# Softmax rows scaled by VectorE instead of GpSimd, and two sets of weight low parts moved the other way

## The chip, the core and the metric

The kernel runs on one core of a Trainium2 chip. Times are device microseconds of one execution of the whole program. Five engines work side by side, each through its own list of instructions in order, and wait for each other by semaphores: TensorE (PE; its weight loads are PEld), VectorE (DVE), ScalarE (ACT), GpSimd (POOL) and SyncE (SP), which issues the DMAs.

## The reference

Two decoder layers on a sequence of 512 tokens with 1024 channels, in float32. Each layer normalises x, projects it once, and runs three groups of causal attention on the parts of the projection:

```python
s = einsum(q, k) * ATTN_SCALE            # 4 forgetting heads, 8 sparse heads, 4 dilated heads
p, _ = masked_softmax(s, mask)           # e / sum(e)
o = einsum(p, v)
o = gb[..., 0:1] * o_c + gb[..., 1:2] * o_s + gb[..., 2:3] * o_w     # the sparse heads: gated sum of three branches
```

The sparse heads have a compressed branch (32 windows of keys and values go through a small MLP with the weights `cmp_w1` and `cmp_w2`), a selected branch and a window branch. With 512 tokens every block is selected and the window covers all, so both run over full causal rows. The heads' outputs are concatenated, multiplied by `w_out`, normalised and added to x. Then comes a gated MLP with a causal convolution, normalised and added likewise.

## The kernel before

**Products in parts.** Every float32 operand of TensorE is parted into a high part, rounded to the type that TensorE takes, and a low part, the rest; a product is three matmuls (high by high, high by low, low by high). For weights `part_weights` (L136) does it: ACT writes the high part of a chunk (L145), and a subtraction writes the low part, raw minus high. It runs on POOL (L149) for the chunks named in `ONPOOL` (L30) and on DVE (L153) for the others, `w1` (compression weights, 16 chunks of 128x1024) and `wo` (the first half of the output weights, 8 chunks) among these. Both cut such a chunk into two halves of 128x512. `plan` lists all chunks in the order of use, and `getw` (L201) asks for the load and the parting of a chunk some chunks ahead of its use (one ahead for these, `PRE`).

**The softmax part.** The full rows (4 forgetting heads, 8 sparse heads with two branches each, 4 dilated heads, each in four tiles of 128 queries: 24 x 4 = 96 units per layer) run as a pipeline of stages, one unit to a slot. The unit of tile t has rows of n = 128(t+1) keys. The stages, with the engine that works and the lag in slots behind the scores:

- `st_scores`: TensorE, two or three matmuls into a bank `s` of PSUM (two banks).
- `st_max`, lag 1: DVE adds the mask and takes the row minimum of the negated scores (L1073), into a row `r` in SBUF; this frees the bank.
- `st_exp`, lag 1: ACT takes the exponential of the row and its sum (L1078).
- `st_norm`, lag 2: DVE takes the reciprocal of the sum (L1083), and POOL multiplies the row by it and by the gate (L1085; by 1.0 where a head has no gate).
- `st_turn`, lag 4: TensorE turns the row's blocks over into a bank `pt` (L1096; two banks).
- `st_keep_hi` and `st_keep_lo`, lag 5: ACT writes the high part of the turned weights (L1113), DVE the low part `pl` (L1118); this frees the bank.
- `st_values` and `st_out`, lag 7: TensorE multiplies with the values into a bank `o` (one bank), ACT and DVE evacuate it (L1153, L1154).

Between the slots' stages TensorE runs pieces of the other projections, of the compression MLP and of the first half of the output projection (`main_pieces`, `cmp_pieces`), 1.4 pieces to a slot at first and 0.8 later. TensorE's order is written out by hand; the other engines' order comes from a scheduler that places instructions by its own estimate of when their inputs are there. DVE also adds up the rotary embedding (L446), POOL also writes low parts of the mixed heads (L642).

Before this part stand the first projections, behind it the rest of the output projection, the norms and the MLP.

Of the kernel before, what the change touches and what calls it, by code (L numbers as in the profile page):

```python
# [13 lines left out]
ALU = mybir.AluOpType  # L14
# [14 lines left out]
TAIL = 4  # L29
ONPOOL = ("dv", "dq", "dk", "ks", "nq0", "kw", "kc", "nq1",  # L30
          (0, "fk", 0), (0, "fk", 1), ("up", 0, 1), ("up", 0, 2), ("up", 0, 3), ("up", 1, 0))
# [9 lines left out]
FIRST = 5  # L41
DCUTS = ("w1", "wo")
EV = (1, 3, 1, 1)
# [30 lines left out]
def tile_hybrid_block(  # L74
# [6 lines left out]
    nc = tc.nc  # L81
# [46 lines left out]

# [1 line left out]
    def load(srcs, nk, ncol, tagn=""):  # L130
# [67 lines left out]
    where = {p[0]: i for i, p in enumerate(plan)}  # L198
    done = [0, 0]

    def getw(*key, ahead=AHEAD, pre=None, peek=False):  # L201
        """the parts of a chunk; has those up to `ahead` after it loaded and those up to `pre` after it parted"""
        i = where[key]
        pre = ahead if pre is None else min(pre, ahead)
        tag = lambda k: "_".join(str(z) for z in k)
        for n in range(len(done)):
            upto = i + (ahead, pre)[n]
            while done[n] < len(plan) and done[n] <= upto:
                k, srcs, nk, ncol, spare = plan[done[n]]
                if n == 0:  # L210
                    ready[k] = load(srcs, nk, ncol, tag(k))
                else:
                    ready[k] = part_weights(ready[k], nk, ncol, spare, tag(k), k[1] in ONPOOL or k[1:4] in ONPOOL or k[0:3] in ONPOOL,
                                            k[1] in DCUTS)
                done[n] += 1
        return None if peek else ready.pop(key)

# [1 line left out]
    epsc = const.tile([128, 1], F32, name="epsc")  # L219
# [4 lines left out]
    def table(func, after):  # L224
        """has the function's table loaded once `after` is there"""
        t = st(1, "tb")
        nc.scalar.activation(t, after, func, scale=0.0, bias=onec)
# [17 lines left out]

    # gains of the pre norms, a channel to a partition: they are applied to the turned rows
    pre_g = const.tile([128, 2, DEPTH, KT], F32, name="preg")
# [7 lines left out]
    def turn_pair(half, i, l, tags, tilewise=False):  # L255
        """two token tiles of h, turned over, times the gains, in two parts"""
        gain = pre_g[:, i, l, :]
        pts = [ps(tag) for tag in tags]
        order = [(k, i) for k in range(KT) for i in range(2)]
        for k, i in sorted(order, key=lambda z: z[1]) if tilewise else order:  # L260
            nc.tensor.transpose(pts[k // 2][:, 256 * (k % 2) + 128 * i:256 * (k % 2) + 128 * i + 128],
                                hs[2 * half + i][:, 128 * k:128 * k + 128], ident)
        for k in range(KT):
            src = pts[k // 2][:, 256 * (k % 2):256 * (k % 2) + 256]
            hi, lo = (z[k // 2][:, k % 2, 256 * half:256 * half + 256] for z in hT)
            nc.scalar.activation(hi, src, AF.Copy, scale=gain[:, k:k + 1])  # L266
            nc.vector.scalar_tensor_tensor(lo, src, gain[:, k:k + 1], f(hi), op0=ALU.mult, op1=ALU.subtract)  # L267

    # post norm, residual and pre norm, in stages, two token tiles at a time
    xs, hs, stats = [], [], {}  # L270

    def post_sq(s, halves, gain, engs, then=None):
        """squares of a token tile, and its products with the gains (the last of them after `then`)"""
        if s % 2 == 0:
            stats["p", s // 2], stats["x", s // 2] = st(4, "sq"), st(2, "sx")
        hs.append(bt([128, DM], name="h"))
        scr = rt()
        for u, y in enumerate(halves):
            cs = slice(512 * u, 512 * u + 512)
            c = 2 * u + s % 2  # L280
            nc.scalar.activation(scr, y, AF.Square, accum_out=stats["p", s // 2][:, c:c + 1])  # L281
            if u == 1 and then is not None:
                then()
            (nc.gpsimd if (s, u) in engs else nc.vector).tensor_mul(hs[s][:, cs], y, gain[:, cs])
# [80 lines left out]

# [1 line left out]
    posi = small.tile([128, NST], I32, tag="posi", bufs=1, name="posi")  # L367
# [57 lines left out]
    for l in range(DEPTH):  # L425
        # ================= mixer =================
        table(AF.Exp, hs[3][:, 0:1])
# [55 lines left out]

# [1 line left out]
        bias = small.tile([128, 28], F32, tag="gbias", bufs=1, name=nm("gbias"))  # L485
# [39 lines left out]
        if l == 0:  # L525
# [3 lines left out]
            nc.vector.tensor_scalar(utri, ui, 0.0, None, op0=ALU.is_ge)  # L529
            # selectors of the forget rows: ones on partitions h and 32 + h  # L530
            pcol = small.tile([128, 4], F32, tag="pc", bufs=1, name="pcol")
# [9 lines left out]

        # log sigmoid(z) = min(z, 0) - log(1 + exp(-|z|))
        lz = zz[:, :, 0:4]
# [41 lines left out]
        if l == 0:  # L585
# [1 line left out]
            dint = rt(dt=I32)  # L587
# [18 lines left out]
            for v, lg in ((2.0, -math.log(2.0)), (3.0, -math.log(3.0))):  # L606
                t = rt()
                nc.vector.tensor_scalar(t, cnt, v, lg, op0=ALU.is_equal, op1=ALU.mult)
                nc.vector.tensor_add(dmask, dmask, t)
            # compressed blocks: valid where q - (16 n + 31) >= 0  # L610
            ci = rt((128, NST, 32))
# [5 lines left out]
            nc.vector.tensor_scalar(cinv, ci, 0.0, BIG, op0=ALU.is_lt, op1=ALU.mult)  # L617
            # heads of a pair: ones on the partitions (32 n ..) of even or of odd n
            odd = const.tile([128, 2], F32, name="odd")
# [24 lines left out]
        def o_mms(o, s, ks, w, first, last):  # L644
            """w: for each of ks its two parts, [128, 1, columns]"""
            sl = slice(128 * s, 128 * s + 128)
# [5 lines left out]

# [1 line left out]
        class Pieces:  # L654
            """`main` pieces in their order; a piece may put off work by some pieces (`later`)"""

# [18 lines left out]
        def proj256(name, evac, after):  # L675
            """[s, 256] columns of w_in, two token tiles to a bank; evac(s, psum) then after()"""
            pp = [ps("acc"), ps("acc")]
# [11 lines left out]
        def staged(key, turned, dup, nh, v=None, plain=0):  # L689
            """evac and after of a group: heads side by side (twice when dup), then turned over"""  # L690
            tl = []
# [34 lines left out]
        def main_pieces():  # L726
            # compressed keys and values
            tl = []
# [84 lines left out]

            # output projection, first its part over the full heads
            for k in OFIRST:
# [19 lines left out]
        def merge(a, b):  # L835
            """two pieces of a to one of b"""
            live = True
# [7 lines left out]

        # the other part of the output projection, over the sparse heads
        ch, po = {}, {}
# [45 lines left out]
        def cmp_pieces(xc, w2r):  # L893
            # gelu and second compression product
            t1, t2 = rt((128, 256)), rt((128, 256))
# [60 lines left out]
            yield  # L956
            # compressed attention weights of all sparse heads
            nq = store["nq"]
# [73 lines left out]

# [1 line left out]
        units = []  # L1034
# [46 lines left out]
        def st_norm(u):  # L1081
            n, row, sm_ = u["n"], u["row"], u["sm"]
            nc.vector.reciprocal(sm_[:, 2:3], sm_[:, 1:2])  # L1083
            g_ = 1.0 if u["gate"] is None else gates[:, u["t"], u["gate"]:u["gate"] + 1]
            nc.gpsimd.tensor_scalar(row[:, 0:n], row[:, 0:n], sm_[:, 2:3], g_, op0=ALU.mult, op1=ALU.mult)  # L1085

        def st_turn(u):
            if u["t"] == 0:
                state["r"] = u["row"]
                return  # L1090
            # the first two tiles of rows share a bank
            blocks = [state["r"][:, 0:128]] if u["t"] == 1 else []
# [67 lines left out]
        def cmp_values(k):  # L1160
            """adds the compressed branch to heads 2k, 2k + 1, both at once"""
            p = ps("pt")
# [22 lines left out]
        with tc.manual_schedule(engines={mybir.EngineType.PE}):  # L1185
# [16 lines left out]
            while whole or live[0] or pieces.late:  # L1202
                if whole and store.get("pc"):
                    cmp_values(whole.pop(0)[0])
                elif live[0] or pieces.late:
                    step()
                    chain_step()
# [1 line left out]
            out_mms(2, (7,), True, (0,))  # L1209
# [28 lines left out]

        # ================= MLP =================
        cw = lambda j, c: cpar[:, j // 2, 44 * (j % 2) + c:44 * (j % 2) + c + 1]  # L1240
# [100 lines left out]
```

## Time and profile before

| | |
|---|---|
| Median of 3 runs | 1392.79 us (1392.07 to 1394.44) |
| Profiled execution, from its first to its last instruction (span) | 1390.7 us |
| TensorE busy | 1343.5 us (97%) |
| DVE busy | 873.2 us (63%) |
| ACT busy | 728.1 us (52%) |
| POOL busy | 311.5 us (22%) |
| Granted TensorE clock, mean | 0.997 |

The page gives the profiled execution's own time as its span; the time of a run also holds what lies around the span. The median lies 2.1 us above the span of the profiled execution. Busy time is the time in which at least one instruction of the engine is in work. A wait is written as the engine and line that waited, an arrow, and what released it. The tile names are the program's: `wl_w` is the low part of a chunk of compression weights, `wl_wo` one of output weights, `pl` a low part of turned softmax weights, `r` a softmax row, `sm` its statistics. The softmax part lies at 70 to 312 us in layer 0 and some 684.6 us later in layer 1.

### The profile page before, as it was taken

Reading aid. Unit: us, or ns where it says so; the run is one execution under the profiler, and the core shown is the slowest. Engines: PE = TensorE matmul, PEld = TensorE weight load, DVE = VectorE, ACT = ScalarE, POOL = GpSimd, SP = SyncE. Lnnn points to the kernel's source line nnn. Section 1 sums busy time; section 2 is a strip of 40 time slices with the busy share of each in tenths; the row PEclk is TensorE's granted clock in tenths of the full one; section 3 lists DMA queues with packets and bytes.
Section 4 is the critical chain, followed back from the end, with each engine's and each line's share of the span. In section 5 each row is a group of like instructions: output and inputs, shape, how many; then the busy total and the mean of one; then the engine's idle time right before and its main releaser. Section 6 shows DMA issues by size and latency. Waiting matters only on the chain.

```text
span 1390.7 us, 21646 instructions
## 1 busy us (share of the span) xinstructions
PE 1343.5 (97%) x8019; PEld 1186.6 (85%) x8019; DVE 873.2 (63%) x2022; ACT 728.1 (52%) x1541; POOL 311.5 (22%) x363
## 2 busy tenths in 40 slices
PE   6999999999999999999999999999989999999997
PEld 6899999987888888888899899999878888888886
DVE  6678778678655555433464887876767555554334
ACT  6567767775443333422465677677755333333222
POOL 1363663345000000000004646633430000000000
PEclk9999999999999999999999999999999999999999
DMA  5223311132233333223323142112313333332231
GB/s 178 77 62 110 108 47 41 50 111 74 75 93 93 104 92 102 96 91 121 118 85 107 47 126 88 32 47 62 107 61 101 97 91 106 92 100 97 91 121 61
DMA packets 145521, 123.78 MB, mean 89 GB/s; under 512 B 8264, under 2 KB 135688, under 8 KB 145416
## 3 DMA queue, kind: packets, MB, share of 16 engines
q1 hardware_dynamic: 145416, 122.40, 29.1%
q8 instruction: 63, 1.03, 0.3%
q14 instruction: 42, 0.34, 0.1%
HBM read 118.19 MB, written 4.19 MB: 88 GB/s over the span
## 4 chain that ended last, share of the span: by engine, by line
PE 79%; DVE 11%; ACT 5%; issue 2%; POOL 1%; DMA 1%; SPq 0%; DVEq 0%; ACTq 0%; POOLq 0%
PE acc L114 35%; PE s L114 17%; PE pt L114 13%; PE o L114 10%; PE pt L1096 3%; DVE wt L771 1%; DVE r L1073 1%; DVE hl L267 1%; DVE x L301 1%; DVE r L446 1%; ACT r L1078 1%; ACT r L281 1%; DMA raw_fv<-in_w_in_dram 1%; DVE pl L1118 1%; ACT hh L266 0%
## 5 line engine op out<-in xcount | busy, mean ns | idle before, releaser
L153 DVE TENSOR_TENSOR wl_up<-raw_up,wh_up 128x1024 fp32r<-128x1024 f32 x78 | 95.5, 1225 | 163.2 <-ACT wh_up L145 163.2
L145 ACT ACTIVATE wh_up<-raw_up 128x1024 fp32r<-128x1024 f32 (+1 forms) x90 | 89.6, 1002 | 156.2 <-PE acc L114 68.2
L153 DVE TENSOR_TENSOR wl_wd<-raw_wd,wh_wd 128x1024 fp32r<-128x1024 f32 x42 | 51.5, 1225 | 133.6 <-ACT wh_wd L145 133.6
L1078 ACT ACTIVATE r<-r,sm 128x128 f32<-128x128 f32 x192 | 107.0, 558 | 25.6 <-DVE sm L1073 22.7
L145 ACT ACTIVATE wh_wd<-raw_wd 128x1024 fp32r<-128x1024 f32 x42 | 44.5, 1060 | 144.9 <-PE pt L114 135.6
L1085 POOL TENSOR_SCALAR r<-r,sm,gates 128x128 f32<-128x128 f32 (+3 forms) x128 | 84.1, 662 | 118.6 <-DVE sm L1083 95.9
L149 POOL TENSOR_TENSOR wl_kc<-raw_kc,wh_kc 128x512 fp32r<-128x512 f32 x8 | 11.3, 1426 | 419.7 <-ACT wh_kc L145 419.7
L114 PE MATMUL acc<-hl,wh_up 128*128 128x512 f32 (+1 forms) x272 | 102.6, 377 | 0.0
L114 PE MATMUL acc<-hh,wh_up 128*128 128x512 f32 (+1 forms) x272 | 102.6, 377 | 0.0
L114 PE MATMUL acc<-hh,wl_up 128*128 128x512 f32 (+1 forms) x272 | 102.5, 377 | 0.0
L114 PE MATMUL s<-k,q 128*128 128x512 f32 (+3 forms) x384 | 98.8, 338 | 2.3 <-DVE k L467 1.0
L1118 DVE TENSOR_TENSOR pl<-pt,ph 128x384 fp32r<-128x384 f32 x144 | 85.5, 594 | 10.2 <-ACT ph L1113 9.1
L1073 DVE CUSTOM_DVE_ANT_0 r<-s,cmask 128x128 f32<-128x128 f32 (+3 forms) x160 | 75.5, 482 | 19.3 <-PE s L114 13.8
L1113 ACT ACTIVATE ph<-pt 128x384 fp32r<-128x384 f32 x144 | 75.3, 523 | 21.3 <-PE pt L1096 19.5
L1096 PE MATMUL pt<-ident,r 128*128 128x128 f32 x480 | 77.2, 275 | 6.8 <-DVE pl L1118 3.3
L114 PE MATMUL acc<-wh_wd,gh 128*128 128x512 f32 x252 | 83.8, 389 | 0.0
L114 PE MATMUL s<-hh,wh_up 128*128 128x512 f32 (+1 forms) x224 | 80.7, 360 | 0.4 <-DVE hl L267 0.4
L114 PE MATMUL s<-hl,wh_up 128*128 128x512 f32 (+1 forms) x224 | 80.4, 359 | 0.0
L114 PE MATMUL s<-hh,wl_up 128*128 128x512 f32 (+1 forms) x224 | 80.4, 359 | 0.0
L1265 ACT ACTIVATE r<-r 128x512 f32<-128x512 f32 x44 | 27.8, 632 | 81.3 <-DVE r L1246 81.0
L114 PE MATMUL o<-ph,v 128*128 128x256 f32 (+1 forms) x288 | 69.6, 270 | 0.4 <-DVE mx L1154 0.4
L114 PE MATMUL o<-pl,v 128*128 128x256 f32 (+1 forms) x288 | 67.2, 282 | 1.9 <-DVE pl L1118 1.7
(431 smaller groups left out, 4227.7 us busy)
## 6 DMA issues: line engine op xcount, KB each, us to landing
raw_up<-in_w_up_dram SPq DMA_DIRECT2D x88, 512.0 KB, 3.8
raw_wd<-in_w_down_dram SPq DMA_DIRECT2D x44, 512.0 KB, 3.5
raw_wo<-in_w_out_dram SPq DMA_DIRECT2D x16, 512.0 KB, 3.5
x<-in_x_dram SPq DMA_DIRECT2D x8, 512.0 KB, 6.7
raw_nq<-in_w_in_dram SPq DMA_DIRECT2D x8, 512.0 KB, 3.8
raw_w<-in_cmp_w_k_dram SPq DMA_DIRECT2D x8, 512.0 KB, 3.7
raw_w<-in_cmp_w_v_dram SPq DMA_DIRECT2D x8, 512.0 KB, 3.7
raw_fk<-in_w_in_dram SPq DMA_DIRECT2D x4, 512.0 KB, 7.1
```

What stands on the lines that cost most here:

```text
L114: nc.tensor.matmul(o, lhsT=lhsT, rhs=rhs, start=start, stop=stop, skip_group_check=True)
L145: nc.scalar.activation(hi[:, ks], raw[:, ks], AF.Copy)
L153: nc.vector.tensor_sub(lo[:, ks], raw[:, ks], f(hi)[:, ks])
L267: nc.vector.scalar_tensor_tensor(lo, src, gain[:, k:k + 1], f(hi), op0=ALU.mult, op1=ALU.subtract)
L281: nc.scalar.activation(scr, y, AF.Square, accum_out=stats["p", s // 2][:, c:c + 1])
L1073: nc.vector.tensor_tensor_reduce(row[:, 0:n], u["S"][:, 0:n], u["mask"][:, 512 - n:512], op0=ALU.add, op1=ALU.min, scale=1.0, scalar=3.0e3 ...
L1078: nc.scalar.activation(row[:, 0:n], row[:, 0:n], AF.Exp, scale=-1.0, bias=sm_[:, 0:1], accum_out=sm_[:, 1:2])
L1085: nc.gpsimd.tensor_scalar(row[:, 0:n], row[:, 0:n], sm_[:, 2:3], g_, op0=ALU.mult, op1=ALU.mult)
L1096: nc.tensor.transpose(p[:, 128 * b:128 * b + 128], src, ident)
L1113: nc.scalar.activation(hi, src, AF.Copy)
L1118: nc.vector.tensor_sub(*u["lo"])
L1265: nc.scalar.activation(cd[0], cd[0], AF.Silu)
```

## The change

`st_norm` has DVE multiply the row, directly behind its reciprocal, where POOL did it. `w1` and `wo` are put into `ONPOOL`, so that POOL makes their low parts in two halves, as DVE did before; `DCUTS`, which had DVE cut these two, is emptied. Comments are taken out elsewhere.

```diff
-ONPOOL = ("dv", "dq", "dk", "ks", "nq0", "kw", "kc", "nq1",
+ONPOOL = ("w1", "wo", "dv", "dq", "dk", "ks", "nq0", "kw", "kc", "nq1",
...
-DCUTS = ("w1", "wo")
+DCUTS = ()
...
-            nc.gpsimd.tensor_scalar(row[:, 0:n], row[:, 0:n], sm_[:, 2:3], g_, op0=ALU.mult, op1=ALU.mult)
+            nc.vector.tensor_scalar(row[:, 0:n], row[:, 0:n], sm_[:, 2:3], g_, op0=ALU.mult, op1=ALU.mult)
```

TensorE's instructions keep their order. On DVE, in the last heads of layer 0 (the dilated ones, about 288 to 296 us before; `r` with a number is the row of one unit, `sm` its statistics, `mx` the sum of a pair of heads), the order changes as follows:

```order
 L1083 RECIPROCAL sm_4240<-sm_4240 128x1
-L1083 RECIPROCAL sm_4256<-sm_4256 128x1
 L1073 ISA r_4283,sm_4284<-s_4249,dmask 128x384
 L1073 ISA sm_4284 128x1
+L1085 TENSOR_SCALAR r_4239<-r_4239,sm_4240 128x128
 L1154 TENSOR_TENSOR mx_4089<-o_4148,r_4274 64x512
 L1118 TENSOR_TENSOR pl_4281<-pt_4270,ph_4280 128x3x128
+L1083 RECIPROCAL sm_4256<-sm_4256 128x1
 L1073 ISA r_4307,sm_4308<-s_4277,dmask 128x512
 L1073 ISA sm_4308 128x1
+L1085 TENSOR_SCALAR r_4255<-r_4255,sm_4256 128x256
```

Each row's scaling stands on DVE some instructions behind its reciprocal, and a later reciprocal has moved behind a low part `pl`.

On POOL, in the stretch where the compression hidden layer runs in layer 0 (about 124 to 145 us before; `wl_w_0_0` and the like are low parts of compression weights, `wl_kw` one of a projection):

```order
-L1085 TENSOR_SCALAR r_1411<-r_1411,sm_1412 128x512
-L1085 TENSOR_SCALAR r_1449<-r_1449,sm_1450 128x128
-L1085 TENSOR_SCALAR r_1486<-r_1486,sm_1487 128x256
+L149 TENSOR_TENSOR wl_w_0_0_275_1556<-raw_w_0_0_234_1380,wh_w_0_0_274_1555 128x512
 L642 TENSOR_TENSOR mix_1508<-mx_1318,mix_1508 128x512
-L1085 TENSOR_SCALAR r_1538<-r_1538,sm_1539 128x384
-L1085 TENSOR_SCALAR r_1641<-r_1641,sm_1642 128x512
+L149 TENSOR_TENSOR wl_w_0_1_282_1597<-raw_w_0_1_273_1553,wh_w_0_1_281_1596 128x512 x2
 L149 TENSOR_TENSOR wl_kw_296_1685<-raw_kw_280_1594,wh_kw_295_1684 128x512 x2
```

The scalings have left POOL's queue, and what stands there now are subtractions of weights and of mixed heads alone.

## Rows read from the trace of the kernel before

**Rows 1.** Page: head, and busy time of each engine.

```profile
span 1390.7 us, 21646 instructions
...
PE 1343.5 (97%) x8019; PEld 1186.6 (85%) x8019; DVE 873.2 (63%) x2022; ACT 728.1 (52%) x1541; POOL 311.5 (22%) x363
```

**Rows 2.** Busy time by stretch: length, then each engine; the two softmax parts.

```profile
70.00:312.00 242.00, 233.53 (x1844) 222.56 (x1843) 188.95 (x618) 175.06 (x470) 122.48 (x152) 1.00 0.25 74
755.00:997.00 242.00, 232.06 (x1832) 220.92 (x1831) 189.20 (x608) 173.46 (x464) 122.22 (x152) 1.00 0.25 73
```

**Rows 3.** Waits of TensorE: total us, times, longest.

```profile
PE pt L712 <- DVE pl L1118: 4.7, 4, 2.5
PE pt L1096 <- DVE pl L1118: 3.3, 2, 1.7
PE pt L1096 <- DVE sm L1083: 2.2, 2, 1.2
PE pt L114 <- DVE pl L1118: 2.0, 2, 1.0
```

**Rows 4.** Groups of instructions: busy us, mean ns of one | idle before.

```profile
L153 DVE TENSOR_TENSOR wl_w<-raw_w,wh_w 128x512 fp32r<-128x512 f32 x32 | 23.9, 762 | 0.0
L153 DVE TENSOR_TENSOR wl_wo<-raw_wo,wh_wo 128x512 fp32r<-128x512 f32 x16 | 13.0, 826 | 0.1
...
L149 POOL TENSOR_TENSOR wl_nq<-raw_nq,wh_nq 128x512 fp32r<-128x512 f32 x16 | 20.5, 1291 | 17.9 <-ACT wh_nq L145 17.7
```

**Rows 5.** POOL's scalings (L1085) by stretch, layer 0.

```profile
70.00:312.00 242.00, 60.34 (x96) 1.00 0.25 74
90.00:110.00 20.00, 4.38 (x8) 1.00 0.25 77
150.00:210.00 60.00, 14.64 (x25) 1.00 0.24 70
284.00:306.00 22.00, 9.01 (x16) 1.00 0.16 49
```

**Rows 6.** Groups of instructions, by form: DVE's tensor by scalars within SBUF.

```profile
L605 DVE TENSOR_SCALAR dmask<-r 128x512 f32<-128x512 f32 x1 | 0.4, 415 | 0.0
L615 DVE TENSOR_SCALAR cvalid<-r 128x128 f32<-128x128 f32 x1 | 0.2, 219 | 0.0
```

**Rows 7.** Busy time by stretch: PE, PEld, DVE, ACT, POOL; DVE's fullest stretches.

```profile
90.00:110.00 20.00, 18.69 (x152) 18.02 (x152) 17.49 (x54) 13.11 (x38) 13.16 (x14) 1.00 0.25 77
150.00:210.00 60.00, 58.05 (x480) 56.48 (x479) 47.09 (x172) 42.09 (x118) 40.31 (x54) 1.00 0.24 70
284.00:306.00 22.00, 18.89 (x127) 16.00 (x126) 18.53 (x61) 20.69 (x55) 14.02 (x20) 1.00 0.16 49
```

**Rows 8.** The same stretches, DVE's compression weight lows alone, and their sum.

```profile
90.00:110.00 20.00, 1.60 (x2) 1.00 0.25 77
...
sum 102.00, DVE 1.60; mean DVE 0.53
```

**Rows 9.** Timeline of DVE and POOL, single places: start, us, instruction.

```profile
152.30 0.22 DVE L446 TENSOR_TENSOR r<-rope,rope 128x64 f32<-128x64 f32 x1
...
112.09 1.10 DVE L446 TENSOR_TENSOR r<-rope,rope 128x64 f32<-128x64 f32 x1
...
111.82 1.28 POOL L642 TENSOR_TENSOR mix<-mx,mix 128x512 fp32r<-128x512 f32 x1 [1.80 <-ACT mix L641]
...
329.13 1.42 DVE L319 TENSOR_SCALAR h<-x,sm 128x1024 f32<-128x1024 f32 x2
...
329.98 4.17 POOL L149 TENSOR_TENSOR wl_up<-raw_up,wh_up 128x512 fp32r<-128x512 f32 x3 [2.36 <-ACT wh_up L145]
```

**Rows 10.** Chain of waits, 284 to 312 us: start, us, what.

```profile
287.34 1.15 issue
288.49 1.27 POOL r L1085 x2
...
291.07 0.57 DVE pl L1118
```

## The prediction, made before the changed kernel ran

> **What bounds the kernel now.** I read the head of the page first. The span is 1390.7 us, TensorE is busy for 1343.5 us of it, DVE for 873.2 and GpSimd (POOL) for 311.5 [rows 1]. So little is to be won: nothing in the change touches a matmul, and only the 47 us in which TensorE is idle can shrink. The change works in the softmax part of each layer, so I next asked for busy time in the two stretches that hold it: 242 us per layer, TensorE 233.5 and 232.1 us, DVE 189.0 and 189.2, POOL 122.5 and 122.2 [rows 2]. The layers are copies of each other to a few tenths; I work on layer 0 and double. Then the waits of TensorE: what ends them in this part is almost always DVE, mostly its low parts `pl` (4.7, 3.3 and 2.0 us); only 2.2 us in two waits stand against the reciprocal, that is, against the normalisation behind it [rows 3]. So the normalisation as such is rarely late. What makes TensorE wait is DVE, an in-order engine, being behind with everything.
>
> **The change, part by part.** DVE loses the low parts of 32 chunk halves of the compression weights (23.9 us) and 16 of the output weights (13.0 us): 36.9 us in all, 18.5 per layer. POOL loses 192 scalings and gains these 48 subtractions. It takes 1.29 us for a subtraction of 128x512 (the `wl_nq` row, the same shape) [rows 4], so it gains 62 us; the 96 scalings of layer 0 alone are 60.3 us [rows 5]. DVE gains the 192 scalings. DVE runs the same form, a tensor by scalars within SBUF, once at 128x128 in 0.22 us and at 128x512 in 0.415 [rows 6]. On the line between them 128x256 is 0.284 and 128x384 0.349; the four shapes are equally frequent, so the mean is 0.317 us, 30.4 us per layer. That is 11.9 us more DVE work per layer than is taken off, on 189. Spread evenly this would fit into 242 us. It does not come evenly: the weight lows sit where TensorE works through the compression hidden layer and the output projection, the scalings sit wherever rows run.
>
> So I sum DVE over the stretches where it is fullest [rows 7], with the scalings that begin there [rows 5]:
> - 90 to 110 us: 17.49 busy, less two weight lows (1.60 [rows 8]), plus 8 x 0.317 = 2.5: 18.4 of 20.
> - 150 to 210 us: 47.09 busy, no weight low to lose [rows 8], plus 25 x 0.317 = 7.9: 55.0 of 60.
> - 284 to 306 us, the last heads, where few projection matmuls are left as filling: 18.53 plus 16 x 0.317 = 5.1: 23.6 of 22. Here the work alone is 1.6 us over the stretch. ACT is at 20.69 of 22 there and stays so.
>
> **The shared port** is the unknown cost. In the trace, DVE's rope sum of 128x64 takes 0.22 us at 152.3; at 112.1 it takes 1.10, and it ends with a POOL subtraction that began 0.27 us earlier and lasts 1.28 [rows 9]. So a DVE instruction with two SBUF inputs stands still until POOL's is through. For the form that the change adds no row shows DVE being held; the nearest is the scaling of 128x1024 at 329.1: there three POOL subtractions that start in the middle of it take 4.17 us instead of 3 x 1.29 = 3.87, so one of them was held by it for some 0.3 us [rows 9]. I bound the price: from nothing (DVE's scaling never waits) to a full hold in the order of arrival, that is the share of time in which POOL is busy after the change, times half a subtraction (0.65 us). POOL's remaining work is 13.16 - 4.38 + 2 x 1.29 = 11.4 of 20 us (57%), 25.7 of 60 (43%) and 5.0 of 22 (23%) [rows 5, 7]. That gives 8 x 0.57 x 0.65 = 3.0, 25 x 0.43 x 0.65 = 7.0 and 16 x 0.23 x 0.65 = 2.4 us. Below nothing the bound hardly goes: what POOL's scalings now hold up on DVE is in the busy time of the stretches already, and I leave it there. I take half of the upper end, since one row shows the hold at full length, the other only a third of a microsecond, and that on the other engine.
>
> The Trainium skill speaks against this change. In "SBUF — State Buffer", section "Who interferes with whom", it says that DVE and GpSimd share one pair of SBUF ports as an exclusive lock held for the whole instruction, and that a `tensor_scalar` in a two-port mode takes it as much as an operation with two SBUF inputs does; "VectorE: DVE Perf Modes", section "Mode 2×_2P", puts an fp32 `tensor_scalar` within SBUF into that mode. The rope row agrees for two inputs; that DVE's scaling is held too, no row shows. By this rule the full hold would apply and the time would be that of rival 1 below, 1414.6 us; if the scaling never waits, only the last stretch overflows, by 1.6 us less the 0.8 worked out below, and the time would be 1392.8 + 2 x 0.8 = 1394.4 us.
>
> **What of it reaches TensorE.** With half the hold DVE has 19.9 us to do in 20, 58.5 in 60 and 24.8 in 22. In the first two it fits only if DVE never waits for an input, and now it is idle for 2.5 of 20 and 12.9 of 60. The score, transpose and value banks give TensorE a slot or so of freedom, so I take 0.5 and 1.5 us. In the last stretch the excess is 2.8; on the other side the chain there now goes through two of POOL's scalings for 1.27 us, which stand behind a weight low in POOL's queue (the 1.15 us put down as issue), and then through DVE's row minimum and low part [rows 10]. On DVE two scalings take 0.4 to 0.8 us; I set 0.8 us against the excess: 2.8 - 0.8 = 2.0. Sum 4.0 us per layer, 8.0 in all.
>
> What I cost at nothing: the lows of the compression and output weights on POOL take 2.6 us per chunk instead of 1.5. They are asked for one chunk ahead, and POOL in all does less (122.5 - 60.3 + 24 x 1.29 = 93 of 242 us), and no longer stands in its queue waiting for reciprocals. If that cover fails, TensorE waits for a `wl_w` or `wl_wo`, up to 1.3 us a chunk. The MLP, the first projections and the post norms have no instruction of the change in them.
>
> The sum: 1390.7 + 8.0 = 1398.7 us for the span. The median of the runs, 1392.8, lies 2.1 us above the profiled span; with the same 2.1 the forecast is **1400.8 us**.
>
> **Rivals.**
> 1. *The lock in full.* DVE is 1.4, 2.0 and 4.0 us over in the three stretches, and in the last one the 3.5 us in which it waits for ACT and TensorE do not fill up either: 10.9 per layer, 1392.8 + 21.8 = 1414.6 us. For it: the rope row. Against it: POOL's work thins out to 23% just where DVE is fullest. Chance 0.12. (The rule of "SBUF — State Buffer", section "Who interferes with whom", in the Trainium skill would have it so.)
> 2. *Faster: the queue behind the reciprocal goes.* Place: the end of the softmax part and the transposes that wait for rows. POOL, in order, now holds weight lows and mix lows behind scalings that wait for DVE, and scalings behind weight lows; afterwards each engine only queues its own. Price: at best half of TensorE's waits on `pl` and on the reciprocal, 4.7 + 3.3 + 2.2 + 2.0 = 12.2 us [rows 3], so 1392.8 - 6 = 1386.8 us. It decides if DVE's scalings fit into the 3.5 us that DVE is idle in 284 to 306, that is, if they cost under 0.22 us each. For it: part of DVE's idle time there is the wait for the very chain that gets shorter. Against it: DVE is what TensorE waits for, and it gets more work. Chance 0.18.
> 3. *No change.* The extra DVE work falls into its idle time and the banks' slack, and the shorter chain at the end pays for the excess of 1.6: 1392.8 us. For it: without the lock only the last stretch overflows. Chance 0.13.
>
> **How the numbers follow.** My forecast has 0.57, with 1396 to 1409 as its own range: no hold and 1.6 us per layer at the low end, nearly the full hold at the high end. A measurement of this kernel can tell about 0.2% (2.8 us) from no change. Slower is the forecast and rival 1: 0.69; same is rival 3: 0.13; faster is rival 2: 0.18. The range that should hold 8 in 10 has to reach past no change on one side and to rival 1 on the other: 1388 to 1414 us.
>
> **What would show it.** Right: DVE's busy time in the softmax part rises by 12 to 25 us per layer; some of the new scalings take about 1 us instead of 0.2 to 0.4 and end with a POOL subtraction; TensorE's waits on DVE grow most between 284 and 306 us and their counterpart 684.6 us later. Wrong: scalings that all keep 0.2 to 0.4 us (no hold for this form); a softmax part no longer than 242 us with DVE over 200 us busy in it (slack larger than I think); TensorE waiting for `wl_w` or `wl_wo`; or a difference in the MLP.

## The result, and the profile after

The changed kernel takes 1425.72 us (median of 4 runs, 1423.93 to 1427.69) against 1393.62 us for the kernel before in the same session: a ratio of 1.0226, 95% interval 1.0209 to 1.0243. It is slower, as forecast, but by 32 us where 8 had been forecast, and the time lies outside the range of 1388 to 1414.

The head of the page of the kernel after, to be held against [rows 1]:

```profile
span 1425.9 us, 21291 instructions
...
PE 1356.4 (95%) x8019; PEld 1195.4 (84%) x8019; DVE 942.5 (66%) x2166; ACT 730.5 (51%) x1541; POOL 254.8 (18%) x219
```

TensorE issues the same 8019 matmuls in the same order. DVE's busy time has grown by 69.3 us; the prediction's terms give 36 (scalings 60.8, less lows 36.9, plus half the hold, 12.4). POOL has shrunk by 57. TensorE's own busy time has grown by 12.9.

Since TensorE's order is unchanged, the n-th matmul of one trace is the n-th of the other, and the two softmax parts can be cut at the same instructions. Busy time by stretch (length, PE, PEld, DVE, ACT, POOL, granted clock), those parts of the kernel after, 260.5 and 258.0 us long where [rows 2] has 242 each:

```profile
70.60:331.10 260.50, 240.27 (x1843) 226.75 (x1843) 223.99 (x690) 176.42 (x470) 94.12 (x80) 0.98 0.23 68
774.10:1032.10 258.00, 237.03 (x1831) 224.12 (x1830) 222.97 (x679) 174.33 (x464) 94.27 (x80) 0.99 0.23 68
```

Nearly all of the loss is in these two parts: the delay of the n-th matmul is 0.5 us at the head of the first, 19.1 at its end, 19.0 at the head of the second, 35.0 at its end and 35.2 near the end of the program. (The two profiled executions lie 35.2 us apart, the medians 32.) DVE is busy for 224 and 223 us there, 34 to 35 more than before (12 to 25 were to show the prediction right); POOL for 94 (the prediction has 93). In two of the three stretches the prediction worked with, the delay grows by 5.2 (90 to 110 us of the trace before) and 5.7 us (150 to 210), in the third by 3.6 (284 to 306). The prediction has 0.5, 1.5 and 2.0, and wanted the largest growth in the third.

The scalings on DVE, by form (busy us, mean ns); `gates` among the inputs means two operands of one value per partition, `sm` alone means one:

```profile
L1085 DVE TENSOR_SCALAR r<-r,sm,gates 128x512 f32<-128x512 f32 x32 | 22.8, 714 | 0.8
...
L1085 DVE TENSOR_SCALAR r<-r,sm,gates 128x128 f32<-128x128 f32 x32 | 16.7, 523 | 0.7
...
L1085 DVE TENSOR_SCALAR r<-r,sm 128x384 f32<-128x384 f32 x16 | 11.5, 722 | 0.3
...
L1085 DVE TENSOR_SCALAR r<-r,sm 128x128 f32<-128x128 f32 x16 | 5.6, 348 | 0.4
```

[Rows 6] had promised 415 ns at 512 columns and 219 at 128. Two things lie on top. One is in every scaling: where no POOL instruction is in work beside it, the median at 128, 256, 384 and 512 columns is 285, 352, 420 and 477 ns with one per-partition operand and 345, 412, 480 and 543 with two. Over the 192 that is a mean of 0.425 us. The other is the hold: 44 of the 192 begin while a POOL instruction runs. For a scaling that meets a POOL instruction I call excess what it takes beyond the unheld median of the same form plus 40 ns (a margin for the scatter); the sum is 23.9 us. By the same count the rope sums (L446) rise from 12.7 us of excess to 23.3.

Where it hurts most, at 92 to 102 us, rows from the timeline of the kernel after (start, us, engine, instruction, idle before and what ended it):

```profile
91.96 1.28 POOL L778 TENSOR_TENSOR wth<-wt,wth 128x512 fp32r<-128x512 f32 x1 [2.99 <-ACT wth L777]
...
92.01 1.46 DVE L1085 TENSOR_SCALAR r<-r,sm 128x384 f32<-128x384 f32 x1
...
94.70 3.20 POOL L771 TENSOR_TENSOR wt<-r,posT 64x496 f32<-64x496 f32 x2
...
96.72 1.33 DVE L446 TENSOR_TENSOR r<-rope,rope 128x32 f32<-128x32 f32 x2
...
97.98 1.28 POOL L149 TENSOR_TENSOR wl_kw<-raw_kw,wh_kw 128x512 fp32r<-128x512 f32 x1
...
98.16 1.87 DVE L771 TENSOR_TENSOR wt<-r,posT 64x496 f32<-64x496 f32 x1
...
101.83 1.11 PE L712 MATMUL pt<-ident,r 128*128 128x128 f32 x4 [2.94 <-DVE pl L1118]
```

The same place of the kernel before:

```profile
90.69 1.40 DVE L446 TENSOR_TENSOR r<-rope,rope 128x32 f32<-128x32 f32 x2
...
92.63 1.48 DVE L771 TENSOR_TENSOR wt<-r,posT 64x496 f32<-64x496 f32 x1
```

The scaling of 384 columns starts 0.05 us behind POOL's subtraction and takes 1.46 us instead of 0.42; then a rope sum and a window sum are held too, and with everything behind them late TensorE stands still for 2.94 us. In the kernel before a rope sum and a window sum are held at this place as well, and TensorE stands still for 1.3 us; new here are the scalings. The row `pl` names the last thing it waited for, not the cause.

TensorE's waits in the kernel after (total us, times, longest), against [rows 3]:

```profile
PE pt L712 <- DVE pl L1118: 6.6, 4, 2.9
...
PE pt L1096 <- DVE sm L1083: 5.5, 4, 3.1
PE s L114 <- DVE sm L1073: 5.4, 6, 1.6
PE pt L1096 <- DVE pl L1118: 4.6, 4, 1.3
PE pt L1096 <- DVE r L1085: 3.5, 4, 1.4
PE acc L994 <- DVE r L973: 2.9, 2, 1.5
```

These are DVE's, and all that grew are, but for 0.9 us on POOL's `r` (L988). No wait is for a `wl_w` or `wl_wo`, and only 3.5 us are for the scaling itself.

A part of the loss may be TensorE's clock. The column before the last two of a stretch is the granted clock; the first four rows are of the kernel after, the two behind them of before:

```profile
101.00:107.80 6.80, 5.97 (x25) 5.58 (x26) 5.55 (x17) 5.53 (x13) 1.50 (x2) 0.50 0.20 68
240.90:244.30 3.40, 3.40 (x19) 3.40 (x18) 2.50 (x10) 3.08 (x8) 1.72 (x2) 0.50 0.51 154
...
804.10:807.50 3.40, 3.40 (x17) 3.33 (x16) 3.31 (x9) 3.01 (x8) 0.31 (x1) 0.50 0.00 0
1002.10:1005.50 3.40, 3.40 (x16) 3.40 (x17) 3.36 (x13) 1.96 (x5) 1.28 (x1) 0.50 0.02 6
```

```profile
331.50:334.90 3.40, 3.40 (x19) 3.40 (x18) 3.01 (x8) 3.40 (x11) 3.40 (x4) 0.50 0.18 51
101.00:107.80 6.80, 6.80 (x57) 6.47 (x56) 6.13 (x19) 4.93 (x14) 2.47 (x3) 1.00 0.26 91
```

In or right behind stretches in which TensorE was kept waiting (the first fall lies in the wait of 2.94 us above; the longest stall ahead of each of the six falls is 0.7 to 3.1 us), the chip grants 0.50 (1.2 GHz) instead of 1.00 (2.4 GHz). Leaving out the very end of the program, the kernel before has 3.4 us of this, the kernel after 23.9 us in six places (22.84 us of it TensorE is busy). If the 19.4 us of additional busy time at half clock would have taken half at full clock, this is up to 9.7 us of the 32. Time at half clock does not tell the loss by itself: the runs below with the lows alone and with no scaling have 13.7 and 10.2 us of it, and are 2 and 3 us slower than the kernel before.

### The profile page after: what moved, and what is told of

The parts are those of the page before. It is cut to its first block, busy times and chain, and to the rows that moved or that the text cites. A ratio compares the mean times of both kernels' runs of the same rounds, so it can differ in the third digit from the quotient of the medians.

```text
span 1425.9 us, 21291 instructions
## 1 busy us (share of the span) xinstructions
PE 1356.4 (95%) x8019; PEld 1195.4 (84%) x8019; DVE 942.5 (66%) x2166; ACT 730.5 (51%) x1541; POOL 254.8 (18%) x219
## 4 chain that ended last, share of the span: by engine, by line
PE 72%; DVE 19%; ACT 5%; issue 2%; DMA 1%; SPq 0%; POOL 0%; ACTq 0%; DVEq 0%; POOLq 0%
PE acc L114 32%; PE s L114 16%; PE pt L114 12%; PE o L114 8%; DVE r L1085 3%; PE pt L1096 2%; DVE pl L1118 2%; DVE r L1073 2%; DVE r L446 1%; DVE q L460 1%; DVE hl L267 1%; DVE x L301 1%; DVE wt L771 1%; PE pt L712 1%; ACT r L281 1%
## 5 line engine op out<-in xcount | busy, mean ns | idle before, releaser
L1073 DVE CUSTOM_DVE_ANT_0 r<-s,cmask 128x128 f32<-128x128 f32 (+3 forms) x160 | 75.5, 482 | 10.2 <-PE s L114 9.8
L1096 PEld LDWEIGHTS pt<-ident,r 128*128 128x128 f32 x480 | 56.0, 142 | 26.1 <-DVE pl L1118 8.1
L1085 DVE TENSOR_SCALAR r<-r,sm,gates 128x128 f32<-128x128 f32 (+3 forms) x128 | 71.4, 564 | 3.0
L114 PEld LDWEIGHTS s<-k,q 128*128 128x128 f32 x384 | 60.4, 195 | 12.2 <-DVE sm L1073 6.7
```

The costliest lines, as they stand in the source:

```text
L114: nc.tensor.matmul(o, lhsT=lhsT, rhs=rhs, start=start, stop=stop, skip_group_check=True)
L1073: nc.vector.tensor_tensor_reduce(row[:, 0:n], u["S"][:, 0:n], u["mask"][:, 512 - n:512], op0=ALU.add, op1=ALU.min, scale=1.0, scalar=3.0e3 ...
L1085: nc.vector.tensor_scalar(row[:, 0:n], row[:, 0:n], sm_[:, 2:3], g_, op0=ALU.mult, op1=ALU.mult)
L1096: nc.tensor.transpose(p[:, 128 * b:128 * b + 128], src, ident)
```

## The experiments

Ratios are to the kernel before, run on the same chip, with 95% intervals; a difference between two experiments is taken from their ratios times 1394 us. "Excess" is the sum described above. Two explanations are set against each other: by the load theory VectorE's added busy time makes TensorE late, by the hold theory its single operations that are held behind GpSimd's do.

One thing is not the same in all runs. The scheduler places the other engines' instructions anew for each kernel. With the weight lows and the scalings left out of the count, some 60 of VectorE's 1830 stand in another place in the run without scalings than in the kernel after, and 26 in the run with six reciprocals. No run tells what the new order costs by itself.

**One part of the change at a time.** The scalings alone on VectorE (the weight lows as before), and the weight lows alone on GpSimd (the scalings as before):

```diff
 e1_scale_only: before, with
-            nc.gpsimd.tensor_scalar(row[:, 0:n], row[:, 0:n], sm_[:, 2:3], g_, op0=ALU.mult, op1=ALU.mult)
+            nc.vector.tensor_scalar(row[:, 0:n], row[:, 0:n], sm_[:, 2:3], g_, op0=ALU.mult, op1=ALU.mult)
 e2_lows_only: before, with
-ONPOOL = ("dv", ...
+ONPOOL = ("w1", "wo", "dv", ...
-DCUTS = ("w1", "wo")
+DCUTS = ()
```

> The scalings alone are on VectorE; the low parts of the compression and output weights stay there too, as before. Load theory (VectorE's added busy time makes TensorE late): VectorE carries the scalings' free 82 us (192 at 0.425 us mean, from the run after) and gives none of the 36 us of weight lows back, so this is the slowest of the three, about 1440 us. Hold theory (VectorE's operations are held behind GpSimd's 1.3 us subtractions): 48 subtractions of 1.3 us are gone from GpSimd, the scalings' excess over their free price falls from 24 us to about 12, and the time falls below the run after, to about 1412 us.

> The weight lows alone are on GpSimd; the scalings stay there too. Load theory: VectorE sheds 36 us of the before run's 873 and TensorE is no later, 1385 to 1394 us. Hold theory: 48 more subtractions hold VectorE's other operations (rope sums 12.7 us of excess before, 23 after), about 1398 us. Third: GpSimd's own queue, 312 us busy before and 374 now, makes scalings late, and TensorE waits for them: 1400 us or more, with waits of the transposes L1096 for GpSimd's L1085.

Measured: scalings alone 1421.41 us, 1.0195 [1.0178, 1.0212]; lows alone 1396.18 us, 1.0014 [1.0005, 1.0023]. The loss comes with the scalings; moving the lows alone costs 2 us. That lies nearest to the hold theory's 1398: the rope sums' excess rises from 12.7 to 17.4 us. With the scalings alone the excess is 18.7 us in the scalings (12 was expected) and 9.9 in the rope sums, so the hold theory had the sign right (4 us faster than the run after, with intervals that just touch, though DVE has 36 us more of weight lows) and the size too large. The load theory's 1440 fell. DVE is busy for longer than in the run after, and the time is shorter:

```profile
PE 1356.0 (95%) x8019; PEld 1196.7 (84%) x8019; DVE 951.0 (67%) x2214; ACT 731.1 (51%) x1541; POOL 193.8 (14%) x171
```

**The scaling without its per-partition operands.** The run after with

```diff
-            nc.vector.tensor_scalar(row[:, 0:n], row[:, 0:n], sm_[:, 2:3], g_, op0=ALU.mult, op1=ALU.mult)
+            nc.vector.tensor_scalar(row[:, 0:n], row[:, 0:n], 0.5, 1.0, op0=ALU.mult, op1=ALU.mult)
```

> The run after with the reciprocal and the gate left out of the scaling, which multiplies by two constants in their place, the instruction and its place kept. Price theory (each operand that is read from a partition's scalar costs about 65 ns): the scaling falls to 0.219 us at 128 columns and 0.415 at 512, VectorE loses 320 x 65 ns = 21 us, and the time falls by about half of that, to 1415 us. Hold theory: the excess of the scalings behind GpSimd stays at about 24 us and the time at 1420 us or above.

Measured: 1412.92 us, 1.0143 [1.0128, 1.0158]. The view of the line shows the shortest and median scaling:

```profile
L1085 DVE TENSOR_SCALAR r<-r x192: 197/340/1470, 71.3 to 1011.6; 128x128 f32<-128x128 f32 x48, 128x256 f32<-128x256 f32 x48, 128x384 f32<-128x384 f32 x48, 128x512 f32<-128x512 f32 x48
```

Unheld medians are 205, 274, 340 and 407 ns, which is what [rows 6] said. So the first per-partition operand costs some 77 ns and the second some 62. The time fell as the price theory had it (1415). The excess stayed at 22.0 us as the hold theory had it, but that theory's 1420 fell: neither theory covers it alone. Constants also free the scaling from waiting for the reciprocal, so the 12 us are not the operands' price alone.

**No scaling at all**, the run after without the line:

> The run after with the scalings of the softmax rows left out altogether (the weights reach the transposes unnormalised and ungated); the weight lows are on GpSimd. If all of the loss comes with the scalings (price or hold), the time is at or below before, 1375 to 1393 us, and the rope sums' excess behind GpSimd falls to 13 us. If the lows on GpSimd have a share of their own, it stays above 1397 us.

Measured: 1397.49 us, 1.0021 [1.0009, 1.0032]. Against the run after that is 29 us for the scalings; what is left above before is the 2 us of the lows. So on GpSimd the scalings cost TensorE next to nothing: nothing could be won by taking them away from there (1.0021 without them, 1.0014 with them, the lows on GpSimd in both). The rope sums' excess was to fall to 13 us and stays at 20.9: it comes with the added subtractions on GpSimd, not with the scalings.

**Fewer subtractions on GpSimd.** First those of the moved weights, then nearly all are left out (the products take the high part twice, which keeps TensorE's work); then the same omission with the scalings on GpSimd, as a control:

```diff
         if pool:
+            if "w1" in tagn or "wo" in tagn:      # e8, e8c: also "dv", "dq", "dk", "nq1", "kw"
+                return hi, hi
             for a, e in PCUT:
```

> The run after with the low parts of the compression and output weights left out (their products take the high part twice, so TensorE's work keeps its size and GpSimd does not subtract for them). VectorE's own load is that of the run after. Load theory (the scalings' busy time on VectorE, in order, is what makes TensorE late): no change, 1424 to 1428 us. Hold theory: 48 subtractions of 1.3 us are gone that hold scalings and rope sums, their excess falls from 24 and 23 us to under 19 and 10 (those of the run with the scalings alone), and the time to 1410 us or less.

> The run after with nearly all of GpSimd's subtractions for weights beside the softmax rows left out (compression, output, dv, dq, dk, nq1 and kw weights: the high part is used twice). The scalings stay on VectorE. Hold theory: the scalings' excess falls from 24 us to under 6, and the time to about 1402 us. Load theory: 1418 us or more, since VectorE's free load has not changed. In between, the share of each is read off: (1425.7 - time) of the 28 us that the scalings cost in all is the holds'.

> The control to the run with GpSimd's weight subtractions left out: the same omission, the scalings on GpSimd as before. It says what the omission gives by itself. If nothing, 1390 to 1395 us, and the scalings on VectorE without most of the holds cost the 9 us that were seen (1403.7 against 1394). If the omission itself makes the kernel faster, 1380 to 1388 us, and they cost 16 to 24 us, so that holds would be only a part of the loss.

Measured: 1417.27 us, 1.0171 [1.0154, 1.0188]; 1403.65 us, 1.0069 [1.0051, 1.0088]; control 1384.58 us, 0.9926 [0.9909, 0.9942]. The first fell by 8 us, half of what the hold theory wanted, with 19.4 us of excess left in the scalings. The second met 1402, but not for the reason given: the control shows that the omission by itself gives 10 us, so the scalings on VectorE still cost 20 us (1.43%) with GpSimd nearly empty. Their excess is 12.0 us in that run (under 6 was expected), and single long holds are left in it, most of them behind L642, L771 and L778, which the edit did not touch: 128x384 with one operand still has a mean of 683 ns against 420 unheld.

```profile
L1087 DVE TENSOR_SCALAR r<-r,sm 128x384 f32<-128x384 f32 x16 | 10.9, 683 | 0.3
```

**The load without the hold.** The run after with each scaling replaced by three, then six reciprocals of one column, the last into the row:

```diff
-            nc.vector.tensor_scalar(row[:, 0:n], row[:, 0:n], sm_[:, 2:3], g_, op0=ALU.mult, op1=ALU.mult)
+            nc.vector.reciprocal(sm_[:, 0:1], sm_[:, 1:2])     # this line twice, then five times
+            nc.vector.reciprocal(row[:, 0:1], sm_[:, 1:2])
```

> The run after with each scaling replaced by three reciprocals of one column (3 x 0.155 = 0.465 us, against the scaling's free price of 0.425 us), the last of them written into the row, so that the transposes wait for it as for a scaling. The scaling itself is left out. VectorE's load and the chain of a row are as in the run after; what differs is that the reciprocals touch one element of a partition each. Load theory: 1418 us or more, near the run with the scalings alone (1421). Hold theory: if one-column operations are not held behind GpSimd, the 24 us of holds are gone and the time is 1405 us or less, near the run without scalings (1397).

> As the run with three reciprocals in place of each scaling, with six. Three added 44 us to VectorE's busy time over the run without scalings (850 to 894: neighbouring records overlap), against 92 us that the scalings add in the run after; six should add about 87 us. The scaling is left out. Load theory: with the busy time of the run after, 1420 us or more. Hold theory: 1402 to 1410 us, since one-column reciprocals are not held.

Measured: 1401.79 us, 1.0056 [1.0038, 1.0073], and 1411.62 us, 1.0121 [1.0106, 1.0136]. The first was a miss as a design: neighbouring records overlap, so it carries half the load meant. The second carries as much busy time on DVE as the run after:

```profile
PE 1352.7 (96%) x8019; PEld 1192.7 (85%) x8019; DVE 942.8 (67%) x3126; ACT 730.0 (52%) x1541; POOL 252.9 (18%) x219
```

942.8 us against 942.5, in the same place of the same chains, and yet it is 15 us faster (1.0121 against 1.0226). It is 14 us slower than without scalings (1.0021), where VectorE is busy for 850.1 us:

```profile
PE 1343.7 (96%) x8019; PEld 1187.4 (85%) x8019; DVE 850.1 (61%) x1974; ACT 727.5 (52%) x1541; POOL 253.5 (18%) x219
```

Neither theory has it alone (1420 or more, 1402 to 1410): equal busy time is worth half the loss when it comes in small even pieces, with what the changed order adds or takes, and the other half comes only when it arrives as holds.

**Shorter subtractions, nothing left out.** GpSimd's subtractions for weights in four pieces of 256 columns instead of two of 512, in the kernel after and in the kernel before:

```diff
-PCUT = ((0, 2), (2, 4))
+PCUT = ((0, 1), (1, 2), (2, 3), (3, 4))
```

> The run after with each of GpSimd's subtractions cut into four pieces of 256 columns in place of two of 512; nothing is left out. Hold theory, if a held operation of VectorE gets in between two pieces: the longest hold falls from 1.46 us to about 0.8, the excess of scalings and rope sums to half (24 to 12 and 23 to 12 us), and the time to 1405 to 1415 us. If the pieces follow each other too closely for that, or the holds decide nothing: 1424 us or more, since GpSimd has some 110 more instructions to start.

> The kernel before with the same cut into four pieces; nothing is left out. Hold theory: rope sums' 12.7 us of excess and the weight lows' 6.2 halve, and the time falls a little, 1388 to 1393 us, which would beat both kernels. Rival: GpSimd, which has the scalings in its queue too, is later by its added instructions, 1394 to 1400 us.

Measured: after 1405.04 us, 1.0072 [1.0057, 1.0087]; before 1389.69 us, 0.9962 [0.9947, 0.9977]. DVE's and ACT's instructions stand in exactly the same order with and without the cut (2166 and 1541 in the kernel after), so nothing but the length of GpSimd's pieces differs. It gives back 21 of 32 us, though GpSimd is busy for 27 us more. The excess falls to 17.2 us in the scalings and 14.0 in the rope sums, not to the 12 each that were expected:

```profile
PE 1350.9 (96%) x8019; PEld 1192.9 (85%) x8019; DVE 923.0 (66%) x2166; ACT 730.2 (52%) x1541; POOL 282.1 (20%) x351
```

Two places of the timeline of the kernel after with the cut show why, and what is left. Here the scaling gets in when the first piece is through, and takes 0.75 us (0.42 unheld):

```profile
291.37 0.73 POOL L149 TENSOR_TENSOR wl_up<-raw_up,wh_up 128x256 fp32r<-128x256 f32 x1 [1.33 <-ACT wh_up L145]
291.56 0.75 DVE L1085 TENSOR_SCALAR r<-r,sm 128x384 f32<-128x384 f32 x1
```

Behind L778, which is not a weight's and was not cut, it is held as long as in the kernel after:

```profile
90.85 1.29 POOL L778 TENSOR_TENSOR wth<-wt,wth 128x512 fp32r<-128x512 f32 x1 [1.47 <-ACT wth L777]
90.90 1.46 DVE L1085 TENSOR_SCALAR r<-r,sm 128x384 f32<-128x384 f32 x1
```

**All of GpSimd's long operations cut**, the weights' as above and, in halves, L642, L771 and L778:

```diff
-            eng.tensor_sub(d[:, 1, cs], sums[k][:, cs], f(d[:, 0, cs]))
+            for c in (...):                      # two halves of 256 columns on GpSimd
+                eng.tensor_sub(d[:, 1, c], sums[k][:, c], f(d[:, 0, c]))
 and in the same way the tensor_add of win_part and the tensor_sub of win_split
```

> The kernel before with all of GpSimd's long operations cut: the weight subtractions into pieces of 256 columns, and the output mix (L642), the rope sums' windows (L771) and their low parts (L778) into halves. Nothing is left out. Hold theory: VectorE's L771 and L446 are held less, 1386 to 1390 us, at or below the run with the weights alone cut (1389.7). Rival: the longer queue of GpSimd, with the scalings in it, costs what the cut gives, 1391 to 1396 us.

> The run after with the same cuts. With the weights alone cut, the scalings still had 17 us of excess, its longest (1.46 us) behind the uncut L778 and L642. Hold theory: these fall to about 0.8 us, the excess to 12 us or less, and the time to 1398 to 1402 us. Load theory for what is left: six reciprocals, unheld, with 92 us of load cost 14 us over the run without scalings; the scalings' own free load of about 68 us should cost some 10 us, so the time stays at 1404 us or above.

Measured: before with all cuts 1392.5 us, 0.998 [0.997, 0.9989]; after with all cuts 1401.35 us, 1.0044 [1.0029, 1.0059]. The same place of the kernel after, with all cuts:

```profile
91.08 0.74 POOL L783 TENSOR_TENSOR wth<-wt,wth 128x256 fp32r<-128x256 f32 x1 [1.44 <-ACT wth L781]
91.13 0.91 DVE L1090 TENSOR_SCALAR r<-r,sm 128x384 f32<-128x384 f32 x1
```

The longest scaling falls from 1.61 to 1.05 us, the excess to 13.5 (12 or less was expected), and the stretch at 101 to 107.8 us is back at full clock. At half clock are 10.2 us in three places instead of 23.9 in six, one of them:

```profile
976.70:980.10 3.40, 3.40 (x16) 3.40 (x17) 3.36 (x11) 2.42 (x7) 1.54 (x2) 0.51 0.00 0
...
101.00:107.80 6.80, 6.34 (x52) 5.89 (x51) 5.63 (x16) 4.95 (x11) 4.44 (x6) 1.00 0.28 77
```

The hold theory's 1398 to 1402 is met, and the load theory's 1404 or more is not. Against the kernel before with the same cuts the whole change now costs 9 us (1.0044 against 0.998).

The version that beats both kernels is the one before with the weights' subtractions in quarters: 1389.69 us, 5 us below it. Cutting the other operations too gave nothing more there (1392.5 us, where the hold theory wanted 1386 to 1390).

## Why the prediction was right in sign and wrong in size

**What bounds the kernel: right.** Of the waits of TensorE that grew, all but 0.9 us are for DVE; the MLP, the first projections and the post norms have no part in it.

**The lows of compression and output weights on POOL at nothing: right as to the wait.** Alone they cost 0.14%, and TensorE never waits for a `wl_w` or `wl_wo`. Beside the scalings they are not free: moving them makes the run with the scalings alone slower by 4 us, although VectorE sheds 36.9 us by it, while the excess rises from 18.7 to 23.9 us in the scalings and from 9.9 to 23.3 in the rope sums.

**The scaling's own price: a quarter too low.** 0.317 us was read from rows without per-partition operands; with them it is 0.425 us, 10.4 us more per layer for 96. The rows of the right engine and operation were not rows of the right operands. The trace before had one that showed it, and the prediction read it for the hold alone: the scaling of 1024 columns (two of them stand in that row) has one per-partition operand and takes 0.75 us, where the line through [rows 6] gives an estimate of 0.68.

```profile
L319 DVE TENSOR_SCALAR h<-x,sm 128x1024 f32<-128x1024 f32 x13 | 9.4, 751 | 0.2
```

**The hold: near in the mean, in part by luck, and wrong in what it was taken for.** I took half of the full hold, 6.2 us for the 49 scalings of three stretches, 0.127 us each; measured are 23.9 us for 192, 0.124 each. But the same 49 have 1.1, 4.8 and 2.8 us, 8.7 in all, where 1.5, 3.5 and 1.2 had been set; the rest lies in layer 1 and, in layer 0, outside the three stretches, where nothing was set. The Trainium skill's "SBUF — State Buffer", section "Who interferes with whom", says that whoever issues first has the ports for its whole instruction; the scaling of 1.46 us that began 0.05 us behind POOL agrees. I used this to scale a mean. What counts is that the price comes as 0.4 to 1.1 us at once for 33 scalings and as next to nothing for the other 159. I also left out that the 48 new subtractions hold DVE's other operations: 10.6 us more in the rope sums.

**"What of it reaches TensorE" is the step that failed.** It set DVE's added time against its idle time in each stretch, let the idle time take nearly all of it, and came to 4.0 us per layer; measured are 18.6 and 16.0. In the first two stretches, where the added work was said to fit, TensorE lost 5.2 and 5.7 us for a forecast of 0.5 and 1.5. Rival 1 did the same sum with the hold in full, and its 1414.6 us fell short too. Added load reaches TensorE even when it fits: 92.7 us of unheld reciprocals, spread over both layers, cost 14 us where DVE had room for them, in an order on DVE that is not quite the same. And a long hold reaches it much more fully: with the order of DVE and ACT unchanged, shorter pieces on GpSimd gave back 21 us, while DVE's busy time fell by 19.5. My reading, which no run shows by itself, is that the idle time I counted on lies where it does not help, since a late score, low part or rope sum makes the following ones late.

**Not in the prediction at all: the clock.** A stall of TensorE can be paid twice, as the granted clock falls to 0.50 with some of them. In the kernel before the one such stretch was outside the softmax part, and I had read the column of 1.00 as a constant.

The division is, then: of the 32 us that the change costs, 9 are left when GpSimd's pieces are short, and 14 are the price of equal unheld busy time; so 15 (the run with six reciprocals) to 23 us (the run with all cuts) belong to long holds, with what the clock adds to both. The share of the load is the less certain one, since the changed order on VectorE is in it.

How much the clock takes by itself stays open: no run changed it alone, and up to 9.7 us is a reading of rows. Open too is why the run with GpSimd nearly empty still cost 20 us over its control. It is not quite the same comparison as the 9 us of the run with all cuts: its control has no weight lows on VectorE, so VectorE's busy time grows by 75 us there (833.9 to 909.3), and by 52 in the other (864.3 to 916.7). Long holds behind L642 are left in it (5.4 us of its excess), but also in the run with quarters (6.0), which costs 15 us over its own control (1.0072 against 0.9962), so they are not the whole difference.

## What to carry to other kernels

Read the price of an operation from a row with the same kinds of operands, and treat a hold between VectorE and GpSimd as single blocks of the length of the other engine's instruction, not as a mean to be set against idle time. Where an in-order engine feeds TensorE, shortening the pieces on the engine that holds it is cheap and may do more than moving work: here it won 5 us for the kernel before and 21 for the kernel after. And ask of every new stall of TensorE whether the granted clock falls behind it.

## What the runs showed of the hardware that was not expected

- A scaling on VectorE takes 197 to 208 ns at 128 columns with two constants, 285 with one per-partition operand and 345 with two; at 512 columns 407, 477 and 543.
- A held scaling gets in between two neighbouring subtractions of GpSimd: it waits for the piece in work, and the next piece is late by some 0.1 us (0.85 instead of 0.74 us at 292.05). GpSimd pays for the cut with 0.74 to 0.84 us (means of the weights' groups in the softmax part) for 256 columns where 512 took 1.3, some 27 us in all, and the kernel is faster all the same.
- Reciprocals of one column are recorded with medians of 143 to 164 ns, but three of them add 44 us of busy time to DVE for 192 rows, 76 ns each.
